# One weight chunk in four of the up stages split by two GpSimd transfers

## The chip, the cores and the metric

The kernel runs on one core of a Trainium2 chip. The core has a matmul engine (TensorE, PE in the profile; its weight loads are PEld), three engines for elementwise work (VectorE or DVE, ScalarE or ACT, GpSimd or POOL), an engine that mostly issues transfers (SyncE or SP), and 16 DMA engines that all issued transfers share. SBUF is the on-chip memory of 128 partitions, PSUM the banks that matmuls write. The metric is the device time of one execution in microseconds; lower is better.

## The reference

Two layers of a decoder on 256 tokens of width 1024, in float32. Each layer has a mixer (attention over the tokens and over a fixed memory) and then a channel mixer, the part that matters here:

```python
def _sq_relu_mlp(h, w_up, w_down):
    u = jax.nn.relu(h @ w_up)
    return (u * u) @ w_down
...
x = x + _sq_relu_mlp(_rmsnorm(x, a_norm_mlp[i]), a_w_up[i], a_w_down[i])
```

`w_up` is 1024 x 4096, `w_down` 4096 x 1024. Layer A's mixer is differential attention, layer B's a causal attention whose keys and values come from `w_kv`; a last norm follows.

## The kernel before

*Precision.* A float32 product is made of three passes in the type float32r, which TensorE takes in one pass each: an operand x is split into h, x rounded to float32r, and l = x - h, also rounded; the product is h·h + h·l + l·h. So every weight and every activation needs two instructions: a copy that rounds (ScalarE) and a subtraction (VectorE).

*Weight chunks.* All weights lie in `wall`, 192 chunks of 128 x 1024 floats (512 KB) in the order of use. `chunk()` (L319) takes the next: SP loads it into a `w` buffer (L313), ScalarE copies it rounded into a `wh` buffer (L336), VectorE subtracts into a `wl` buffer (L338). There are 4 `w`, 6 `wh` and 6 `wl` buffers, handed out strictly in the order in which the program names them.

*The up stage* (`mlp_up`, L777 on). 16 blocks b of two chunks (mi = 0, 1). `up_chunk` (L814) issues for a chunk 16 matmuls with `wh` (on `xn`'s h and l for each of 8 k) and then 8 with `wl` (L821), into one half of an `acc` bank (4 banks). After two chunks VectorE takes the bank through the relu and the norm's factor `rb` (L790), ScalarE squares (L793) and rounds it (L805), VectorE makes its l (L807). For the blocks 1, 3, 5, 7, 9 and 11 VectorE also makes four sums of blocks (L800 to L803), which the down stage uses.

*Around it.* Before the up stage lies the output projection (`out_proj`, L755, matmuls L765); when one of its banks is done, VectorE adds it to `xT` (L751), and `norm_tile` makes a piece of `xn` from that (ScalarE L352, VectorE L354); ScalarE squares the piece (L451) and GpSimd adds the squares up (L452), from which the norm's factor comes. After it comes the down stage (`natural_down`, matmuls L871), whose `fast_pair` trades an eighth of the products for more splits on ScalarE (L894) and VectorE (L895, L902).

*The order.* Every instruction is a step of a plan (`Plan`, L59). A step has an engine, an estimated duration, what it reads and writes, a `lag` (time after its end until the result can be used) and a priority, its place in the program minus a shift from a table (`EARLY`). `order()` (L118) plays the steps through with these estimates; each engine takes the ready step of the best priority whose buffers are free. The instructions are then issued in the order of the planned starts, and on the chip each engine works through its queue in that order, waiting where it must.

Of the kernel before, what the change touches and what calls it, by code (L numbers as in the profile page):

```python
# [26 lines left out]
CW = 1024  # L27
# [31 lines left out]
class Plan:  # L59
# [1 line left out]


    LAT = 200
    SAME = {"pe": 0, "act": 130, "dve": 130, "pool": 130, "dma": 0}

    def __init__(self, caps, fifo):
        self.caps = caps
# [48 lines left out]
        return st  # L116

    def order(self):  # L118
        look = {"pe": 0, "act": LOOK, "dve": LOOK, "pool": 0, "dma": 0}
        ready = {e: [] for e in self.SAME}  # L120
        idle = {e: 0 for e in self.SAME}
        idle["dma"] = 740
        events = []
        for st in self.steps:
            if st.wait == 0:
                for e, *_ in st.ways:
                    ready[e].append(st)
        heapq.heappush(events, 0)
        heapq.heappush(events, 740)
        releases = []  # L130
        port = 0
        left = len(self.steps)
        done = []
        while left:
            if not events:
                stuck = sorted((x.pri, e, [(b.cls, b.slot) for b in x.bufs]) for e in ready for x in ready[e])
                raise RuntimeError(f"plan stuck, {left} left: {stuck[:6]}")
            t = heapq.heappop(events)
            while events and events[0] <= t:
                heapq.heappop(events)  # L140
            while releases and releases[0][0] <= t:
                _, _, cls, slot = heapq.heappop(releases)
                self.free[cls].append(slot)
            for e in ready:
                if idle[e] > t or not ready[e]:
                    continue
                best, soon = None, None
                for st in ready[e]:
                    if st.start is not None:
                        continue  # L150
                    if not self.fits(st):
                        continue
                    if st.ready <= t:
                        if best is None or st.pri < best.pri:
                            best = st
                    elif st.ready <= t + look[e] and (soon is None or st.pri < soon.pri):
                        soon = st
                if best is None:
                    later = [st.ready for st in ready[e] if st.ready > t]
                    if later:  # L160
                        heapq.heappush(events, min(later))
                    continue
                way = next(x for x in best.ways if x[0] == e)
                if soon is not None and soon.pri < best.pri and t + way[1] > soon.ready + 100:
                    heapq.heappush(events, soon.ready)
                    continue
                st = best
                for e2, *_ in st.ways:
                    ready[e2].remove(st)
                st.start, st.end, st.eng, st.emit = t, t + way[1], e, way[2]  # L170
                if e == "pool" or (e == "dve" and st.port):
                    st.end = port = max(t, port) + way[1]
                for b in st.bufs:
                    if b.slot is None:
                        self.free[b.cls].sort()
                        b.slot = self.free[b.cls].pop(0)
                        if b.cls in self.fifo:
                            self.fifo[b.cls].remove(b)
                    b.left -= 1
                    if b.left == 0:  # L180
                        heapq.heappush(releases, (st.end + st.lag + self.LAT, id(b), b.cls, b.slot))
                        heapq.heappush(events, st.end + st.lag + self.LAT)
                idle[e] = st.end
                heapq.heappush(events, st.end)
                left -= 1
                done.append(st)
                for n in st.succ:
                    n.wait -= 1
                    same = len(n.ways) == 1 and n.ways[0][0] == e
                    n.ready = max(n.ready, st.end + st.lag + (self.SAME[e] if same else self.LAT))  # L190
                    if n.wait == 0:
                        for e2, *_ in n.ways:
                            ready[e2].append(n)
                        heapq.heappush(events, max(n.ready, t))
        self.span = max(st.end for st in done)
        return sorted(done, key=lambda x: x.start)
# [12 lines left out]
def t_act(n, psum=False, scale=False):  # L209
    return (51 if psum else 93) + 0.835 * n + (93 if scale else 0)  # L210
# [15 lines left out]
def tile_hybrid(ctx: ExitStack, tc: tile.TileContext, xa, xb, memt, xnat, mnat, w0, wall, consts, fgain, out):  # L226
# [17 lines left out]
    def buf(cls, shape, dt=F32, pool=None):  # L244
        pool = pool or ring
        return Buf(cls, lambda slot: pool.tile(shape, dt, name=name(cls), tag=f"{cls}{slot}", bufs=1))
# [72 lines left out]
    def chunk(dma_pieces=1):  # L319
        i = st_["i"]  # L320
        st_["i"] += 1
        w = buf("w", [128, CW])
        h = buf("wh", [128, CW], F32R)
        l = buf("wl", [128, CW], F32R)
        hs = (0, 1)
        if dma_pieces == 1:
            dma(lambda: w.t, wall[i], 4 * 128 * CW, w=[(w, 0), (w, 1)])
        else:
            for p in hs:
                dma(lambda p=p: w.t[:, p * 512:(p + 1) * 512], w0[p], 256 * CW, w=[(w, p)], pri=2 * p - 1.5)  # L330
        old, P.shift = P.shift, EARLY["w" + st_["layer"]]
        for p in (hs if st_["pieces"] == 2 else [hs]):
            q = p if isinstance(p, tuple) else (p,)
            sl = slice(q[0] * 512, q[-1] * 512 + 512)
            n = 512 * len(q)
            P.add(("act", t_act(n), lambda sl=sl: nc.scalar.copy(h.t[:, sl], w.t[:, sl])),  # L336
                  [(w, x) for x in q], [(h, x) for x in q])
            P.add(("dve", t_dve(n), lambda sl=sl: nc.vector.tensor_sub(l.t[:, sl], w.t[:, sl],  # L338
                                                                       h.t[:, sl].bitcast(F32))),
                  [(w, x) for x in q] + [(h, x) for x in q], [(l, x) for x in q], port=True)  # L340
        P.shift = old
        return h, l


    class Tiles:

# [427 lines left out]
    def mlp_up(st, sums=()):  # L774

        st.rstd()
        us = [big(i, [128, 4, 2, S], F32R) for i in range(8)]  # L777
        st_["pieces"] = 1
        first = True
        for b in range(16):  # L780
            u = buf("u", [128, 2, S])
            ps = bank("acc")
            for mi in range(2):
                wh, wl = chunk()
                up_chunk(ps, mi, wh, wl)
            if first:
                bcast(st)
                first = False
            k0 = 2 * b % 4
            P.add(("dve", t_dve(512, True), lambda u=u, ps=ps: nc.vector.scalar_tensor_tensor(  # L790
                u.t, ps.t.rearrange("p (a s) -> p a s", a=2), 0.0, rb_t[:, None, :].to_broadcast([128, 2, S]),
                op0=OP.max, op1=OP.mult)), [ps, "rb"], [u])
            P.add(("act", t_act(512), lambda u=u: nc.scalar.activation(u.t, u.t, AF.Square)), [u], [u])  # L793
            if b in sums:
                dst, keys = sums[b]

                def blocks(u=u, dst=dst):
                    a = [u.t[:, k, hf * 128:hf * 128 + 128] for hf in range(2) for k in range(2)]
                    s = [dst()[:, i * 128:i * 128 + 128] for i in range(4)]
                    nc.vector.tensor_add(s[0], a[2], a[3])  # L800
                    nc.vector.tensor_sub(s[1], s[0], a[0])
                    nc.vector.tensor_sub(s[2], a[0], a[2])
                    nc.vector.tensor_sub(s[3], a[1], s[1])  # L803
                P.add(("dve", 4 * t_dve(128) + 100, blocks), [u], keys, port=True)
            P.add(("act", t_act(512), lambda u=u, t=us[b // 2], k0=k0: nc.scalar.copy(t.t[:, k0:k0 + 2, 0], u.t)),  # L805
                  [u], [(us[b // 2], b)])
            P.add(("dve", t_dve(512), lambda u=u, t=us[b // 2], k0=k0: nc.vector.tensor_sub(  # L807
                t.t[:, k0:k0 + 2, 1], u.t, t.t[:, k0:k0 + 2, 0].bitcast(F32))), [u, (us[b // 2], b)],
                [(us[b // 2], b, 1)], port=True)
        return us  # L810
# [591 lines left out]
```

## Time and profile before

| | |
|---|---|
| three runs | 599.97 us median (599.6 to 600.78) |
| profiled execution, first to last instruction | 725.8 us |
| TensorE clock granted in it | 0.755 of full |
| busy in it: PE, DVE, ACT, POOL | 716.6, 491.3, 398.0, 54.4 us |
| up stages in it | 145.4 to 257.4 and 503 to 615 us |
| read from HBM | 106.72 MB |

The profiled execution has no time of its own beside its span; it is one execution at a lower TensorE clock than the timed ones can have had, as the span is longer than they took. A row of a group reads: line, engine, operation, output and inputs with shapes, count, then busy time and mean ns of one, then the idle time of the engine just before them and what ended it. In an order of time each row starts with start and duration in us, and ends with the idle time before it and its releaser in brackets.

### The profile page before, as it was taken

The page shows a single profiled execution, that of the slowest core. Times are in us where ns is not written, and L with a number is a line of the kernel's source. Part 1 is how long each engine was busy: PE and PEld are TensorE (multiplying, and loading weights), DVE is VectorE, ACT ScalarE, POOL GpSimd, SP SyncE. Part 2 cuts the span into 40 slices and gives each one's busy share as a digit, 9 for nine tenths or more (in the row PEclk, how much of TensorE's full clock was granted, in tenths as well). Part 3 has the DMA queues.
Part 4 walks back from the last instruction along what each step waited for, and adds up shares of the span by engine and source line. Part 5 has one row for each costly group of instructions (what it writes and reads, how often), then busy time and mean ns, then how long its engine had stood idle before and what let it go on. Part 6 is the DMA issues. An engine that isn't in the chain of part 4 may idle for free.

```text
span 725.8 us, 10368 instructions
## 1 busy us (share of the span) xinstructions
PE 716.6 (99%) x3794; PEld 590.5 (81%) x3794; DVE 491.3 (68%) x871; ACT 398.0 (55%) x750; POOL 54.4 (8%) x67
## 2 busy tenths in 40 slices
PE   9999999999999999999999999999999999999996
PEld 7676769999999977677777776889999999776775
DVE  5777666587556687766776577675675666876664
ACT  6776666455544554444575477656464455554422
POOL 0121110030000000000111121001200000000002
PEclk8777777777777777777777777777777777777777
DMA  8854432435444433546455432224444443354421
GB/s 303 293 183 165 146 95 79 145 119 175 151 168 146 152 139 132 188 145 209 139 174 179 169 120 85 88 88 143 153 164 152 154 158 125 127 186 151 148 85 59
DMA packets 30003, 108.45 MB, mean 149 GB/s; under 512 B 3328, under 2 KB 3328, under 8 KB 29696
## 3 DMA queue, kind: packets, MB, share of 16 engines
q1 hardware_dynamic: 29664, 107.26, 43.4%
q8 instruction: 30, 0.49, 0.3%
q10 hardware_dynamic: 288, 0.52, 0.2%
q14 instruction: 21, 0.17, 0.1%
HBM read 106.72 MB, written 1.05 MB: 148 GB/s over the span
## 4 chain that ended last, share of the span: by engine, by line
PE 98%; DVE 1%; DMA 1%; ACT 0%; issue 0%; SPq 0%; ACTq 0%
PE acc L821 30%; PE acc L499 23%; PE t L871 23%; PE acc L765 7%; PE acc L871 6%; PE t L586 2%; PE t L624 2%; PE t L681 1%; PE t L557 1%; DMA xT<-xa 1%; PE t L1013 0%; PE t L990 0%; DVE xT L751 0%; PE t L579 0%; PE t L721 0%; PE t L720 0%
## 5 line engine op out<-in xcount | busy, mean ns | idle before, releaser
L336 ACT CAST wh<-w 128x512 fp32r<-128x512 f32 (+1 forms) x232 | 182.5, 814 | 191.3 <-PE acc L821 74.0
L338 DVE TENSOR_TENSOR wl<-w,wh 128x512 fp32r<-128x512 f32 (+1 forms) x232 | 213.4, 939 | 86.7 <-ACT wh L336 71.7
L821 PE MATMUL acc<-xn,wh 128*128 128x256 f32 x1024 | 157.3, 314 | 0.5 <-DVE xn L354 0.5
L821 PEld LDWEIGHTS acc<-xn,wh 128*128 128x128 f32 x1024 | 150.7, 224 | 0.7 <-DVE xn L354 0.7
L871 PE MATMUL t<-wh,B 128*128 128x512 f32 (+1 forms) x368 | 134.4, 453 | 0.0
L499 PE MATMUL acc<-wh,xn 128*128 128x512 f32 x256 | 101.6, 472 | 0.7 <-ACT xn L352 0.7
L871 PEld LDWEIGHTS t<-wh,B 128*128 128x128 f32 x368 | 72.5, 199 | 29.8
L821 PE MATMUL acc<-xn,wl 128*128 128x256 f32 x512 | 84.1, 314 | 0.0
L871 PE MATMUL t<-wl,B 128*128 128x512 f32 (+1 forms) x184 | 82.9, 450 | 0.0
L821 PEld LDWEIGHTS acc<-xn,wl 128*128 128x128 f32 x512 | 78.1, 224 | 0.0
L499 PEld LDWEIGHTS acc<-wh,xn 128*128 128x128 f32 x256 | 51.0, 199 | 23.5 <-issue 2.2
L765 PE MATMUL acc<-B,wh 128*128 128x256 f32 x256 | 60.1, 323 | 0.0
L499 PE MATMUL acc<-wl,xn 128*128 128x512 f32 x128 | 58.0, 453 | 0.0
L790 DVE SCALAR_TENSOR_TENSOR u<-acc,rb 128x512 f32<-128x512 f32 x32 | 21.9, 690 | 50.5 <-PE acc L821 50.5
L871 PEld LDWEIGHTS t<-wl,B 128*128 128x128 f32 x184 | 37.0, 201 | 15.1
L765 PEld LDWEIGHTS acc<-B,wh 128*128 128x128 f32 x256 | 46.3, 216 | 0.9 <-issue 0.8
L452 POOL TENSOR_TENSOR sqa<-sqa,sq 128x256 f32<-128x256 f32 x21 | 20.3, 966 | 295.7 <-ACT sq L451 294.9
L765 PE MATMUL acc<-B,wl 128*128 128x256 f32 x128 | 40.0, 313 | 0.0
L895 DVE TENSOR_TENSOR wl<-wsum,wh 128x1024 fp32r<-128x1024 f32 x24 | 29.4, 1223 | 8.9 <-ACT wh L894 6.5
L533 POOL TENSOR_TENSOR ropet<-ropes,consts 128x256 f32<-128x256 f32 (+1 forms) x28 | 25.1, 917 | 129.0 <-ACT ropes L522 106.5
L499 PEld LDWEIGHTS acc<-wl,xn 128*128 128x128 f32 x128 | 26.8, 210 | 9.1
L894 ACT CAST wh<-wsum 128x1024 fp32r<-128x1024 f32 x24 | 25.3, 1052 | 15.9 <-PE acc L871 6.9
(223 smaller groups left out, 899.1 us busy)
## 6 DMA issues: line engine op xcount, KB each, us to landing
w<-wall SPq DMA_DIRECT2D x191, 512.0 KB, 3.3
w<-memt SPq DMA_DIRECT2D x4, 512.0 KB, 5.0
B<-xnat SPq DMA_DIRECT2D x1, 1024.0 KB, 7.4
B<-mnat SPq DMA_DIRECT2D x1, 1024.0 KB, 8.9
xT<-xa SPq DMA_DIRECT2D x1, 540.0 KB, 3.8
w<-w SPq DMA_DIRECT2D x2, 256.0 KB, 3.5
xT<-xb SPq DMA_DIRECT2D x1, 512.0 KB, 6.6
consts<-consts SPq DMA_DIRECT2D x1, 256.5 KB, 4.5
```

What stands on the lines that cost most here:

```text
L336: P.add(("act", t_act(n), lambda sl=sl: nc.scalar.copy(h.t[:, sl], w.t[:, sl])), [(w, x) for x in q], [(h, x) for x in q])
L338: P.add(("dve", t_dve(n), lambda sl=sl: nc.vector.tensor_sub(l.t[:, sl], w.t[:, sl], h.t[:, sl].bitcast(F32))), [(w, x) for x in q] + [(h, ...
L452: P.add(("pool", t_pool(S), lambda: nc.gpsimd.tensor_tensor(self.acc.t, self.acc.t, sq.t, op=OP.add)), [sq, self.acc], [self.acc])
L499: nc.tensor.matmul(pss[hf].t[:, c0:c1], a(k)[:, ts], b.t[:, o + c0:o + c1], start=(k == 0 and i == 0), stop=(k == KT - 1 and i == 2))
L533: nc.gpsimd.tensor_tensor(t.t[:, 0:nh, e:e + 32], zs.t[:, 0:nh, 32 - e:64 - e], b(sin[:, e:e + 32]), op=OP.mult)
L586: nc.tensor.matmul(sp[hd].t[:, c], qk[a].t[r, qb * 128:(qb + 1) * 128], qk[b].t[r, S:S + c.stop - c.start], start=(qb == 0 and i == 0 and ...
L765: nc.tensor.matmul(o, a.t[:, ws], x(k), start=(n == 0 and m % 2 == 0 and i == 0), stop=(n == KT - 1 and i == 2), skip_group_check=True)
L790: P.add(("dve", t_dve(512, True), lambda u=u, ps=ps: nc.vector.scalar_tensor_tensor(u.t, ps.t.rearrange("p (a s) -> p a s", a=2), 0.0, rb_ ...
L821: nc.tensor.matmul(ps.t[:, o], w.t[:, k * 128:(k + 1) * 128], xnt[:, k, x], skip_group_check=True, **flags)
L871: nc.tensor.matmul(ps.t[:, c0:c1], x, y, start=start and i == 0, stop=stop and i == 2, skip_group_check=True)
L894: P.add(("act", t_act(m), lambda: nc.scalar.copy(h[x].t[:, :m], src())), keys, [h[x]])
L895: P.add(("dve", t_dve(m), lambda: nc.vector.tensor_sub(l[x].t[:, :m], src(), h[x].t[:, :m].bitcast(F32))), keys + [h[x]], [l[x]], port=True)
```

## The change

In the odd blocks of both up stages the second chunk, so one in four, 16 in all, comes from a new function `added_chunk` instead of `chunk`. GpSimd issues a transfer of the chunk straight into the `wh` buffer (source float32, destination float32r, so it rounds). ScalarE multiplies `wh` by -1 into the `wl` buffer. GpSimd issues a second transfer of the same chunk that adds onto `wl`, which then holds the chunk less its rounded copy. No `w` buffer, no SP transfer and no subtraction on VectorE belong to such a chunk. In the plan the two transfers are steps of a queue of their own ("sw", 1300 ns each, lags 2500 and 3000), though they are issued on GpSimd's queue as its additions are. The steps of a chunk stay three.

```diff
-    SAME = {"pe": 0, "act": 130, "dve": 130, "pool": 130, "dma": 0}
+    SAME = {"pe": 0, "act": 130, "dve": 130, "pool": 130, "dma": 0, "sw": 0}
...
-        look = {"pe": 0, "act": LOOK, "dve": LOOK, "pool": 0, "dma": 0}
+        look = {"pe": 0, "act": LOOK, "dve": LOOK, "pool": 0, "dma": 0, "sw": 0}
...
+    def added_chunk():
+
+        i = st_["i"]
+        st_["i"] += 1
+        h = buf("wh", [128, CW], F32R)
+        l = buf("wl", [128, CW], F32R)
+        hk, lk = [(h, 0), (h, 1)], [(l, 0), (l, 1)]
+        P.add(("sw", 1300, lambda: nc.gpsimd.dma_start(h.t, wall[i])), (), hk, lag=2500)
+        old, P.shift = P.shift, EARLY["w" + st_["layer"]]
+        P.add(("act", t_act(CW), lambda: nc.scalar.mul(l.t, h.t.bitcast(F32), -1.0)), hk, lk)
+        P.shift = old
+        P.add(("sw", 1300, lambda: nc.gpsimd.dma_start(l.t, wall[i], accum_op=OP.add)), lk, lk, lag=3000)
+        return h, l
...
-                wh, wl = chunk()
+                wh, wl = added_chunk() if mi and b % 2 else chunk()
```

## The prediction

> **What bounds the kernel now.** I read the page's busy times, clock line and chain first, then the table of stages, then the waits inside an up stage, and last the order of time around one added chunk.
>
> ```profile
> span 725.8 us, 10368 instructions
> ...
> PE 716.6 (99%) x3794; PEld 590.5 (81%) x3794; DVE 491.3 (68%) x871; ACT 398.0 (55%) x750; POOL 54.4 (8%) x67
> ...
> PE 98%; DVE 1%; DMA 1%; ACT 0%; issue 0%; SPq 0%; ACTq 0%
> ...
> L336 ACT CAST wh<-w 128x512 fp32r<-128x512 f32 (+1 forms) x232 | 182.5, 814 | 191.3 <-PE acc L821 74.0
> L338 DVE TENSOR_TENSOR wl<-w,wh 128x512 fp32r<-128x512 f32 (+1 forms) x232 | 213.4, 939 | 86.7 <-ACT wh L336 71.7
> ```
>
> TensorE is busy for 716.6 of 725.8 us and 98% of the chain of work that ended last is its own; 9.2 us are all it idles. The two split instructions wait for others (last figures of their rows): the cast on ScalarE for TensorE to release a buffer, the subtraction on VectorE for the cast. The work that the change takes from VectorE is work that follows TensorE. The stages (window, length, then busy time and instructions of PE, PEld, DVE, ACT and POOL, granted clock, share of the DMA engines, GB/s):
>
> ```profile
> 145.40:165.50 20.10, 19.61 (x139) 19.38 (x138) 15.58 (x32) 11.41 (x21) 7.07 (x7) 0.75 0.37 132
> 165.50:257.40 91.90, 91.90 (x649) 91.90 (x649) 59.74 (x87) 46.55 (x58) 0.00 (x0) 0.75 0.47 155
> ...
> 523.10:615.00 91.90, 91.90 (x650) 91.90 (x649) 59.74 (x87) 46.31 (x58) 0.00 (x0) 0.75 0.46 155
> ```
>
> ```profile
> core 0: 725.8 us, clock 0.755
> ```
>
> The up stages are 145.4 to 257.4 and about 503 to 615. In their main stretches TensorE has no gap at all, VectorE is busy 65% and ScalarE 51%, and GpSimd does nothing. The granted clock was 0.755 (last row, the table of cores), and this is why the span says 725.8 while the runs took 599.97: TensorE's 716.6 us are 541 us at full clock (716.6 x 0.755). In the timed runs the clock must lie between 0.92 (541 over 599.97 less the 9.2 idle) and 1. I make the sum on the profiled execution as a difference and add it to 599.97; where a term depends on TensorE's pace I recompute it for clock 1. There VectorE's 59.74 us face 69.4 us of TensorE (91.90 x 0.755), 86%: still not the bound.
>
> **The change part by part.** Per added chunk (16 in all, 8 per up stage: every fourth) one SP transfer and one VectorE subtraction go; the cast on ScalarE becomes a multiplication by -1 of the same tile size; two GpSimd transfers of 512 KB come, one before and one after it. The groups, and below them a wait, in the first layer's main stretch (165.5 to 257.4):
>
> ```profile
> L338 DVE TENSOR_TENSOR wl<-w,wh 128x1024 fp32r<-128x1024 f32 x24 | 29.3, 1220 | 3.9 <-PE acc L821 2.7 <-ACT wh L336 0.7
> L336 ACT CAST wh<-w 128x1024 fp32r<-128x1024 f32 x23 | 24.2, 1051 | 29.5 <-PE acc L821 29.5
> ```
>
> ```profile
> DVE u L790 <- PE acc L821: 23.9, 12, 2.1
> ```
>
> *Subtraction removed:* 16 x 1.22 = 19.5 us off VectorE. In the main stretch VectorE then waits 8 x 1.22 us longer for TensorE; u (L790) already waits 23.9 us for TensorE's acc there. Worth to TensorE: 0. *Cast replaced:* 16 x 1.05 us out, the same in (nearest row: the cast itself; below it nothing, above it the 1.22 of the subtraction): 0, hidden under ScalarE's 29.5 us of waiting. *SP transfer removed:* the SP queue has 16 issues fewer; the next chunk's load takes the free w buffer earlier and then waits for TensorE as the cast did: 0.
>
> *Two transfers on GpSimd's queue.* The trace has none, so I bound them by the issue table (median us from issue to landing last).
>
> ```profile
> w<-wall SPq DMA_DIRECT2D x191, 512.0 KB, 3.3
> w<-memt SPq DMA_DIRECT2D x4, 512.0 KB, 5.0
> B<-xnat SPq DMA_DIRECT2D x1, 1024.0 KB, 7.4
> B<-mnat SPq DMA_DIRECT2D x1, 1024.0 KB, 8.9
> xT<-xb SPq DMA_DIRECT2D x1, 512.0 KB, 6.6
> ```
>
> The rounding transfer has the bytes and source of the first row: 3.3 to 6.6 us, and I take 4.2, between the rows of 3.3 and 5.0, as it is issued by another engine but in the same traffic. The adding transfer also reads its destination, so as many bytes again: 3.3 (the read is free) to 8.9 (the slowest 1 MB row), and I take 7.4, the other 1 MB row. What an issue takes of GpSimd itself has no row; it stands idle in the stretch (0.00 above), so it lengthens the chain at most. Extra traffic is 16 x 0.52 MB on 108, beside DMA engines that are 47% busy in the stage: 0. The Trainium skill, "Collectives: The Full Stack", section "The bandwidth ceiling", says that a reducing transfer is slower because the add needs two source reads, about half the rate; doubling the first row would make it 6.6 us and the chain below 11.9. No row here shows it, and the sum stays the same by either.
>
> What must hide them is the lead of the ring of six wh and six wl buffers (TensorE's and ScalarE's order of time, start and duration first, and a piece of the chain).
>
> ```profile
> 192.56 2.44 PE L821 MATMUL acc<-xn,wh 128*128 128x256 f32 x16
> 194.84 1.28 PE L821 MATMUL acc<-xn,wl 128*128 128x256 f32 x8
> ```
>
> ```profile
> 195.04 1.05 ACT L336 CAST wh<-w 128x1024 fp32r<-128x1024 f32 x1 [2.35 <-PE acc L821]
> ```
>
> ```profile
> 165.47 91.95 PE acc L821 x648
> ```
>
> A chunk is 24 matmuls, 16 with wh and then 8 with wl; 91.95 / 648 x 24 = 3.41 us. The cast at 195.04 starts just when a chunk's 16 wh matmuls end (192.56 + 2.44 = 195.0): a wh buffer comes free there, and it is read again by the sixth chunk after, whose wl is wanted six whole chunks later: 6 x 3.41 = 20.4 us, and 15.4 us at clock 1. Its wh is wanted 16 matmuls earlier, 18.2 and 13.7 us. The chain in that time is 4.2 + 1.05 + 7.4 = 12.7 us, at the low ends 7.7, at the high ends 16.6; its first half alone, at most 6.6, is far inside 13.7. Hidden, with 2.7 us left at clock 1. The multiplication waits on ScalarE's queue for the first transfer, with casts of the next chunks and u's squares behind it; they too have five chunks of lead, and four acc banks stand between u and TensorE. Cost 0.
>
> *GpSimd's queue.* The adding transfer waits there for ScalarE. Behind it can stand the adds of squares at the head of the stage.
>
> ```profile
> 155.12 1.49 POOL L452 TENSOR_TENSOR sqa<-sqa,sq 128x256 f32<-128x256 f32 x1 [0.56 <-ACT sq L451]
> ```
>
> ```profile
> POOL sqa L452 <- ACT sq L451: 294.9, 10, 196.2
> ```
>
> The last of them ends at 156.6 us, then GpSimd is idle for 196.2 us, so in the stage nothing is behind the transfers. At the head the adds feed the reciprocal root that u needs; u's first step runs some 10 us later, with TensorE in about its sixth chunk (145.4 + 6 x 3.41 = 165.9) and acc banks for eight: 7 us of room. Cost 0, at most a few tenths.
>
> *The head of the stage* is the one place without that lead.
>
> ```profile
> 139.84 1.05 ACT L336 CAST wh<-w 128x1024 fp32r<-128x1024 f32 x1 [2.08 <-PE acc L765]
> 143.23 1.05 ACT L336 CAST wh<-w 128x1024 fp32r<-128x1024 f32 x1 [2.34 <-PE acc L765]
> 144.54 1.36 ACT L352 ACTIVATE xn<-xT 128x256 fp32r<-128x256 f32 x3 [0.26 <-DVE xT L751]
> ...
> 495.91 1.05 ACT L336 CAST wh<-w 128x1024 fp32r<-128x1024 f32 x1 [2.34 <-PE acc L765]
> ```
>
> ```profile
> 149.79 3.79 PE L821 MATMUL acc<-xn,wh 128*128 128x256 f32 x25 [0.49 <-DVE xn L354]
> ```
>
> Casts of up chunks 0 to 5 run ahead of the stage; counted from the first, the one at 139.84 is chunk 3's, the first that is added. Its buffer is free at about 139.8; the multiplication can start when the transfer has landed, and 4.70 us after 139.84 ScalarE begins the eight xn pieces on which TensorE's first up matmuls wait (149.79: it does wait for xn, through VectorE). If the multiplication stands ahead of xn in ScalarE's order, xn is held once the transfer takes more than 4.70 - 1.05 = 3.65 us, at clock 1 more than 4.70 x 0.755 - 1.05 = 2.5. If it stands behind them nothing is held, as chunk 3's wl is wanted some 13 us into the stage. What is late next if xn comes later is VectorE's own run of adds and xn remainders, already continuous from 144.1 to 152.3, so it hides part. I take 0 here and carry the rest as a rival. The subtractions that fall away near the head (chunk 3's, right after 139.84, in idle time) give nothing either.
>
> Sum: 0 + 0 + 0 + 0: 725.8 for the profiled execution, **600.0** for the runs. What a measurement of this kernel tells from no change is about 0.2%, 1.2 us: 598.8 to 601.2.
>
> **The rivals.** *ScalarE is held at the head (slower).* At 4.2 us xn comes 0.55 us late per layer at the profile's clock and 1.7 at clock 1; at 6.6 us it is 2.95 and 4.1. Over two layers, with VectorE hiding none: 601.1 to 608.2, and 603.4 at my value and clock 1. For: the buffer frees only 4.70 us ahead of xn, in both layers. Against: order behind xn, or VectorE's own run. Beside it, the Trainium skill, "GPSIMD Engine Reference", section 2.1, says the first call of a freshly loaded GpSimd routine pays some 6 us; on the first transfer that would be about 9.3 us and would hold xn by up to 6.8 once. No row shows such a load.
>
> *The chain outlasts the ring (slower).* Decides at 15.4 us (clock 1). At the high ends, 16.6, each of 16 chunks is late by 1.2: 619; with 8.9 for both transfers 18.9, late by 3.5: 655. For: nothing like the adding transfer is in the trace. Against: it would have to take over 10 us for 512 KB, more than the slowest 1 MB row.
>
> *VectorE was a bound in the timed runs (faster).*
>
> ```profile
> 146.40:157.40 11.00, 10.51 (x75) 10.28 (x74) 8.79 (x14) 6.59 (x15) 7.07 (x7) 0.75 0.28 100
> 157.40:168.30 10.90, 10.90 (x80) 10.90 (x79) 8.56 (x20) 4.34 (x5) 0.00 (x0) 0.75 0.58 196
> 168.30:179.20 10.90, 10.90 (x79) 10.90 (x78) 8.47 (x17) 8.40 (x12) 0.00 (x0) 0.75 0.48 151
> ```
>
> ```profile
> 158.23 1.23 DVE L338 TENSOR_TENSOR wl<-w,wh 128x1024 fp32r<-128x1024 f32 x1 [2.21 <-PE acc L821]
> ```
>
> In the first 33 us VectorE is busy 78 to 80%; at clock 1 these windows are 8.2 to 8.3 us long and VectorE, with 8.5 to 8.8, is the longer. Two subtractions per layer (chunks 7 and 11; the one at 158.23 is of that time) leave it: at most 4 x 1.22 = 4.9, so 595.1; half of it, 597.5, if the ring hides the rest. A better order of the later stages, which the changed times also shift, would show the same sign. Against: the rings and banks let TensorE run on for five chunks, and 158.23 begins after a wait of 2.21.
>
> **How the numbers follow.** Hidden 0.38; held at the head 0.28; chain too long 0.09; VectorE was a bound 0.25. A slight holding within 1.2 us counts as no change (0.02 of the 0.28). So faster 0.25, same 0.40, slower 0.35. The forecast is the likeliest, 600.0, its own range 598.8 to 601.2. The range of 8 in 10 runs from 596.5, leaving 0.05 of the VectorE case, to 606.0, leaving the long chain (0.09) and the dearest part of the head (0.04).
>
> **What would show it.** Right: both up stretches still 91.9 us at the same clock, no idle time of PE L821 on wl, VectorE's busy time 19.5 us less and its waits longer by as much, GpSimd with 32 issues. Head right: the first xn on ScalarE still some 4.7 us after the third-last wh release. Wrong: PE idle before L821 with the new transfers as releaser (chain), ScalarE idle ahead of L352 until a GpSimd transfer (head), or shorter heads of both up stages (VectorE). A timed difference with equal profiles would put it on the clock that the profile doesn't have.

## The result: 1.4% slower, in the two up stages

The changed kernel took 606.91 us (median of 4 runs, 603.88 to 610.17), the kernel before 599.79 beside it (598.34 to 600.78): ratio 1.0136, 95% interval 1.0088 to 1.0183. The forecast was no change, 600.0, with a range up to 606.0, so it was wrong in kind and in size.

The profile of before on which the prediction rests had a granted clock of 0.755. A second profile of the same kernel, taken with the first experiments (c1), had 0.997 and belongs to a run of 597.4 us. Nearly all timed runs of before have clocks of 0.994 to 0.999, so it is the one to compare with. Page of that profile of before, first lines:

```profile
span 595.6 us, 10368 instructions
...
PE 582.2 (98%) x3794; PEld 513.2 (86%) x3794; DVE 485.2 (81%) x871; ACT 390.7 (66%) x750; POOL 56.0 (9%) x67
```

Page of the changed kernel (that run took 610.17 us), with the groups of the split instructions and the transfers (median us from issue to landing last):

```profile
span 608.4 us, 10367 instructions
...
PE 593.1 (97%) x3794; PEld 523.6 (86%) x3794; DVE 467.5 (77%) x855; ACT 387.6 (64%) x750; POOL 80.3 (13%) x99
...
L338 DVE TENSOR_TENSOR wl<-w,wh 128x512 fp32r<-128x512 f32 (+1 forms) x216 | 194.7, 924 | 48.7 <-ACT wh L336 48.1
L336 ACT CAST wh<-w 128x512 fp32r<-128x512 f32 (+1 forms) x216 | 164.9, 798 | 79.3 <-PE t L885 29.2
...
L354 ACT ACTIVATE wl<-wh 128x1024 fp32r<-128x1024 f32 x16 | 17.0, 1060 | 35.1 <-DMA wh<-wall 29.4
...
w<-wall SPq DMA_DIRECT2D x175, 512.0 KB, 4.3
wh<-wall POOLq DMA_DIRECT2D x16, 512.0 KB, 6.7
wl<-wall POOLq DMA_DIRECT2D x16, 512.0 KB, 5.7
```

(Up to L344 the changed kernel has the same line numbers; behind the new function every line stands 14 later, so the xn of L352 and L354 is L366 and L368, the up matmul L821 is L835, out_proj's L765 is L779. Inside the function L352 is the rounding transfer, L354 the multiplication by -1, L356 the adding transfer.)

VectorE has 17.7 us less to do, and TensorE is busy 10.9 us longer with the same 3794 matmuls. The 16 multiplications wait for their rounding transfers (29.4 us in all), whose landing takes 6.7 us in the median, not the 4.2 that the prediction took. Measured from the end of out_proj's last matmul to the first matmul of the down stage, the up stages are

| | layer A, us | layer B, us | rest of the span |
|---|---|---|---|
| before (at 0.997) | 89.54 | 90.10 | 416.0 |
| after | 93.10 | 97.54 | 417.8 |
| after, second and third profile | 94.73, 93.79 | 95.62, 96.73 | 414.7, 415.2 |

The rest of the span did not gain from VectorE's relief. In the first of these profiles 11.0 of the 12.8 us lie in the two up stages; the other 1.8 come ahead of the first added chunk, where TensorE waited 2.22 us at 32.67 us and the granted clock fell behind it (0.78, 0.50 and 0.87 in the windows of 2 us from 32 to 38), which before's profile does not have. In the second and third the up stages are longer by 10.7 and 10.9 us.

**The head.** Chain of the changed kernel, head of layer A's up stage and then of layer B's:

```profile
122.22 4.51 DMA wh<-wall
126.72 0.02 issue
126.75 1.06 ACT wl L354
127.81 0.41 ACT xn L366
...
414.93 7.04 DMA wh<-wall
421.96 0.02 issue
421.99 1.06 ACT wl L354
423.04 0.41 ACT xn L366
```

ScalarE's order of time there, layer B, after:

```profile
417.54 1.05 ACT L336 CAST wh<-w 128x1024 fp32r<-128x1024 f32 x1 [4.71 <-PE acc L779]
421.99 1.06 ACT L354 ACTIVATE wl<-wh 128x1024 fp32r<-128x1024 f32 x1 [3.40 <-DMA wh<-wall]
422.95 2.49 ACT L366 ACTIVATE xn<-xT 128x256 fp32r<-128x256 f32 x6
```

and in before at clock 0.997:

```profile
413.44 1.31 ACT L352 ACTIVATE xn<-xT 128x256 fp32r<-128x256 f32 x3
```

The multiplication of the first added chunk stands ahead of xn in ScalarE's queue, waits 3.40 us for its transfer, and xn with it. In before xn begins 1.7 us ahead of the end of out_proj (413.44 against 415.11; in layer A 124.32 against 125.98). In after it begins at its end in layer A (127.71 against 127.65) and 2.6 us behind it in layer B (422.95 against 420.38): held by 1.7 and 4.2 us. TensorE's order of time, after, layer A and layer B:

```profile
128.26 4.98 PE L835 MATMUL acc<-xn,wh 128*128 128x256 f32 x37 [0.61 <-ACT xn L366]
...
423.49 4.52 PE L835 MATMUL acc<-xn,wh 128*128 128x256 f32 x22 [2.23 <-ACT xn L366]
```

After the gap in layer B the granted clock itself falls (table of windows; the figure ahead of the last two is the clock):

```profile
420.00:424.00 4.00, 1.64 (x13) 1.21 (x11) 0.98 (x4) 2.01 (x4) 0.65 (x1) 1.00 0.20 69
424.00:428.00 4.00, 3.98 (x22) 3.85 (x23) 4.00 (x9) 3.95 (x11) 2.01 (x3) 0.71 0.74 131
428.00:432.00 4.00, 4.00 (x32) 4.00 (x31) 1.95 (x3) 3.10 (x6) 2.08 (x3) 0.87 0.42 133
```

Windows of half a us show how: the clock is at one half from about 425.7 to 429.1 us, some 3.4 us, and full before and behind. Its two ends:

```profile
425.50:426.00 0.50, 0.50 (x5) 0.50 (x5) 0.50 (x3) 0.50 (x3) 0.00 (x0) 0.65 0.86 147
...
428.50:429.00 0.50, 0.50 (x4) 0.50 (x3) 0.50 (x2) 0.10 (x1) 0.42 (x2) 0.50 0.30 41
429.00:429.50 0.50, 0.50 (x6) 0.50 (x5) 0.50 (x1) 0.50 (x2) 0.42 (x1) 0.94 0.90 213
```

4 x 0.29 + 4 x 0.13 = 1.7 us of matmul time are lost there beside the 2.2 of waiting.

**The step.** The long pieces of the chain in the main stretches, before at clock 0.997:

```profile
142.23 73.45 PE acc L821 x648
...
431.92 73.46 PE acc L821 x648
```

and after:

```profile
144.82 76.09 PE acc L835 x646
...
441.76 76.32 PE acc L835 x648
```

There is no gap in either and the clock is 1.00 in both, yet a matmul comes every 113.3 ns (73.45 / 648) in before and every 117.8 in after: 2.9 us per stretch. So in this profile the 11.0 us are 5.7 for this step, and what is left, 0.7 in layer A and 4.6 in layer B, is the head's: in layer B 2.2 of waiting and 1.7 of clock make most of it (in layer A before had waited 1.05 us for VectorE anyway). The split is this execution's: the step comes out otherwise in others, before's included (below).

### The profile page after: what moved, and what is told of

Read it like the earlier page. It is cut to its first block, busy times and chain, and to the rows that moved or that the text cites. A ratio compares the mean times of both kernels' runs of the same rounds, so it can differ in the third digit from the quotient of the medians.

```text
span 608.4 us, 10367 instructions
## 1 busy us (share of the span) xinstructions
PE 593.1 (97%) x3794; PEld 523.6 (86%) x3794; DVE 467.5 (77%) x855; ACT 387.6 (64%) x750; POOL 80.3 (13%) x99
## 3 DMA queue, kind: packets, MB, share of 16 engines
HBM read 115.11 MB, written 1.05 MB: 191 GB/s over the span
## 4 chain that ended last, share of the span: by engine, by line
PE 90%; DMA 5%; ACT 2%; DVE 2%; issue 1%; SPq 0%; ACTq 0%
PE acc L835 29%; PE t L885 22%; PE acc L513 19%; PE acc L885 6%; PE acc L779 6%; PE t L600 2%; DMA wh<-wall 2%; PE t L638 2%; DMA w<-wall 2%; PE t L695 1%; DMA w<-memt 1%; PE t L571 1%; DVE wl L338 1%; DVE xn L368 1%; DMA xT<-xa 1%
## 5 line engine op out<-in xcount | busy, mean ns | idle before, releaser
L338 DVE TENSOR_TENSOR wl<-w,wh 128x512 fp32r<-128x512 f32 (+1 forms) x216 | 194.7, 924 | 48.7 <-ACT wh L336 48.1
L336 ACT CAST wh<-w 128x512 fp32r<-128x512 f32 (+1 forms) x216 | 164.9, 798 | 79.3 <-PE t L885 29.2
L835 PE MATMUL acc<-xn,wh 128*128 128x256 f32 x1024 | 134.1, 283 | 3.5 <-ACT xn L366 2.8
L835 PEld LDWEIGHTS acc<-xn,wh 128*128 128x128 f32 x1024 | 126.4, 190 | 4.8 <-ACT xn L366 3.3
L885 PE MATMUL t<-wh,B 128*128 128x512 f32 (+1 forms) x368 | 111.9, 386 | 0.0
L513 PE MATMUL acc<-wh,xn 128*128 128x512 f32 x256 | 86.2, 404 | 0.8 <-ACT xn L366 0.6
L835 PE MATMUL acc<-xn,wl 128*128 128x256 f32 x512 | 70.5, 280 | 0.0
L835 PEld LDWEIGHTS acc<-xn,wl 128*128 128x128 f32 x512 | 64.6, 189 | 0.0
L779 PE MATMUL acc<-B,wh 128*128 128x256 f32 x256 | 50.8, 289 | 0.0
L807 ACT ACTIVATE u<-u 128x512 f32<-128x512 f32 x32 | 20.2, 630 | 40.0 <-DVE u L804 40.0
L779 PEld LDWEIGHTS acc<-B,wh 128*128 128x128 f32 x256 | 41.1, 191 | 0.6 <-issue 0.5
L354 ACT ACTIVATE wl<-wh 128x1024 fp32r<-128x1024 f32 x16 | 17.0, 1060 | 35.1 <-DMA wh<-wall 29.4
L779 PE MATMUL acc<-B,wl 128*128 128x256 f32 x128 | 36.1, 282 | 0.0
L821 DVE TENSOR_TENSOR B<-u,B 128x512 fp32r<-128x512 f32 x32 | 22.0, 687 | 13.8 <-ACT B L819 13.8
L619 ACT ACTIVATE B<-t,nm 128x128 f32<-128x128 f32 (+1 forms) x64 | 27.2, 443 | 4.6 <-DVE nm L615 2.7
```

The costliest lines, as they stand in the source:

```text
L354: P.add(("act", t_act(CW), lambda: nc.scalar.mul(l.t, h.t.bitcast(F32), -1.0)), hk, lk)
L513: nc.tensor.matmul(pss[hf].t[:, c0:c1], a(k)[:, ts], b.t[:, o + c0:o + c1], start=(k == 0 and i == 0), stop=(k == KT - 1 and i == 2))
L619: nc.scalar.activation(p[hd].t[:, c], sp[hd].t[:, c], AF.Exp, bias=nm[hd][:, qb:qb + 1], accum_out=ss[:, hd, qb:qb + 1])
L779: nc.tensor.matmul(o, a.t[:, ws], x(k), start=(n == 0 and m % 2 == 0 and i == 0), stop=(n == KT - 1 and i == 2), skip_group_check=True)
L835: nc.tensor.matmul(ps.t[:, o], w.t[:, k * 128:(k + 1) * 128], xnt[:, k, x], skip_group_check=True, **flags)
L885: nc.tensor.matmul(ps.t[:, c0:c1], x, y, start=start and i == 0, stop=stop and i == 2, skip_group_check=True)
```

## The experiments

Ratios are to the kernel before on the same chip, which took 596.93 (first four rows), 597.6 (e4, e5), 598.55 (e7, e8) and 597.49 us (last three).

| run | us | ratio, 95% interval |
|---|---|---|
| e1 multiplication behind xn | 611.43 | 1.0244 (1.0210 to 1.0279) |
| e2 without the first added chunk | 599.03 | 1.0025 (1.0006 to 1.0044) |
| e3 only the first added chunk | 604.55 | 1.0117 (1.0086 to 1.0148) |
| c1 before, profiled | 597.4 | one run |
| e4 plan with longer landings | 607.58 | 1.0162 (1.0122 to 1.0203) |
| e5 before, ScalarE held | 606.67 | 1.0137 (1.0106 to 1.0169) |
| e6, e9 after; c2 before | 606.83, 607.51; 595.89 | one run each |
| e7 before, eight interruptions | 603.97 | 1.0095 (1.0063 to 1.0126) |
| e8 subtractions away | 600.89 | 1.0042 (1.0017 to 1.0067) |
| e10 before, one interruption a stage | 602.74 | 1.0068 (1.0034 to 1.0102) |
| e12 before, two a stage | 602.21 | 1.0058 (1.0027 to 1.0088) |
| e11 after, one a stage | 605.32 | 1.0117 (1.0066 to 1.0167) |

**Which chunk costs it: e2 and e3.** The 16 added chunks are parted into the first of each stage and the other 14.

```diff
-                wh, wl = added_chunk() if mi and b % 2 else chunk()
+                wh, wl = added_chunk() if mi and b % 2 and b > 1 else chunk()   # e2
+                wh, wl = added_chunk() if mi and b == 1 else chunk()            # e3
```

> The first added chunk of each up stage goes through the old path, 14 stay. Head theory: 598 to 601, the second added chunk's transfer has the whole ring as its lead. Even theory and traffic theory: 14/16 of the loss stays, about 606.

> Only the first added chunk of each up stage, 2 in all. Head theory: 604 to 608, nearly all of the loss, with xn late in both layers. Even theory and traffic theory: 2/16 of the loss, about 600.7.

Without the first one the kernel is 0.25% slower than before; the first one alone costs 1.2%. Together 1.4%, as measured. In e2 both heads are those of before (TensorE waits for xn only 1.1 us, in layer A, on VectorE), and its up stages are 90.57 and 90.37 us, so 1.0 and 0.3 us longer. In e3 the head of layer B is held again, by a wait of 2.0 us. Its up stages are 89.89 and 96.90 us: nearly all of the loss is in layer B, where the main stretch also runs at the slow step (75.85 us for 644 matmuls), so e3's 1.2% is not the head alone.

**The other order: e1.** A longer lag for the first rounding transfer puts the multiplication behind xn.

```diff
-        P.add(("sw", 1300, lambda: nc.gpsimd.dma_start(h.t, wall[i])), (), hk, lag=2500)
+        P.add(("sw", 1300, lambda: nc.gpsimd.dma_start(h.t, wall[i])), (), hk, lag=9000 if late else 2500)   # late: b == 1
```

> All 16 added chunks stay; only the first one of each up stage gets a longer lag in the plan (9000 in place of 2500), which puts its multiplication behind the xn pieces in ScalarE's order. Head theory (ScalarE's queue is held at the head of each up stage by the first transfer, some 7 us in all): 599 to 601, the first xn within 1 us of its add in both layers, no TensorE gap there. Even theory (each of the 16 chunks costs about 0.45 us through the chain or through traffic): 606 to 607, unchanged. Traffic theory (the SP loads are slowed by the adding transfers): 606 to 607.

A miss: it is slower by another percent. xn is early again (123.15 us, out_proj ends at 124.82), but now the adding transfer is late. GpSimd's order of time in layer A, e1:

```profile
119.39 0.74 POOL L352 DMA_DIRECT2D wh<-wall  x1 [3.42 <-PE acc L779]
125.17 1.55 POOL L466 TENSOR_TENSOR sqa<-sqa,sq 128x256 f32<-128x256 f32 x2 [5.04 <-ACT sq L465]
128.78 3.48 POOL L466 TENSOR_TENSOR sqa<-sqa,sq 128x256 f32<-128x256 f32 x2 [2.07 <-ACT sq L465]
132.21 0.89 POOL L356 DMA_DIRECT2D wl<-wall  x1
```

and TensorE's:

```profile
141.18 2.08 PE L835 MATMUL acc<-xn,wl 128*128 128x256 f32 x8 [4.45 <-DMA wl<-wall]
```

The adding transfer is issued at 132.21 behind the adds of squares, which wait for ScalarE, and lands 8.9 us later (the median in this run is 5.6); TensorE stands 4.45 us for it. Ahead of xn the first added chunk holds xn, behind it its own wl is late: neither order was free.

**A plan with longer landings: e4.** The plan's two transfers get other issue times and lags: the rounding one now takes 7.0 us in the plan (measured in after: 6.7 in the median), the adding one 8.5, which is nearer to the 8.9 of e1's head than to the median of 5.7.

```diff
-        P.add(("sw", 1300, lambda: nc.gpsimd.dma_start(h.t, wall[i])), (), hk, lag=2500)
+        P.add(("sw", 600, lambda: nc.gpsimd.dma_start(h.t, wall[i])), (), hk, lag=6400)
...
-        P.add(("sw", 1300, lambda: nc.gpsimd.dma_start(l.t, wall[i], accum_op=OP.add)), lk, lk, lag=3000)
+        P.add(("sw", 900, lambda: nc.gpsimd.dma_start(l.t, wall[i], accum_op=OP.add)), lk, lk, lag=7600)
```

> All 16 added chunks, with the durations and lags of the two transfers in the plan set to what the first trace shows (600 + 6400 and 900 + 7600 in place of 1300 + 2500 and 1300 + 3000), nothing else. If the head loss comes of the order alone (multiplication ahead of xn, and in the run with the multiplication behind xn TensorE's wl matmuls too early in its queue): 597 to 601. If the adding transfer at the head can't be in time in any order: 603 or more, with TensorE waiting for wl there.

The wait for xn at the head is gone, and the time is not: three waits for wl (1.9 us together), two for u (1.5) and one for the adds of squares (0.7) took its place, and the slow step came in parts of both stretches. The profiled run is the quickest of six (605.21 us). With these lags the chain had no room; whether lags nearer to the medians would do better was not tried.

**The hold without the transfers: e5.** In before, the cast of the same chunk is done six times over, so ScalarE is held, and no transfer is changed.

```diff
-            P.add(("act", t_act(n), lambda sl=sl: nc.scalar.copy(h.t[:, sl], w.t[:, sl])),
+            P.add(("act", t_act(n), lambda sl=sl: [nc.scalar.copy(h.t[:, sl], w.t[:, sl]) for _ in range(times)]),   # times: 6 if b == mi == 1
```

> The kernel before, no GpSimd transfer; only the cast of the fourth chunk of each up stage is done six times on ScalarE (five for nothing), which ends some 2.7 us after the time at which xn would start. Head theory (what costs is that xn is held on ScalarE): 601 to 608, TensorE stalls of 1 to 3 us at both heads. Rival (the transfers themselves cost): 597 to 600, since the five casts fall into idle time of ScalarE. If the slow step of TensorE (118 in place of 113 ns per matmul for a whole up stage) follows a disturbed head, at least one of the two up stages has it here.

It is as slow as the changed kernel. Waits, windows and chain of e5, and between them VectorE's row ahead of xn:

```profile
PE acc L821 <- ACT xn L352: 5.8, 2, 2.9
```

```profile
125.98 1.23 DVE L338 TENSOR_TENSOR wl<-w,wh 128x1024 fp32r<-128x1024 f32 x1 [6.86 <-ACT wh L336]
```

```profile
128.00:132.00 4.00, 3.73 (x17) 3.18 (x18) 4.00 (x10) 4.00 (x11) 1.47 (x2) 0.77 0.40 133
132.00:136.00 4.00, 3.99 (x28) 3.70 (x28) 4.00 (x7) 2.20 (x6) 2.57 (x4) 0.80 0.40 131
424.00:428.00 4.00, 4.00 (x24) 4.00 (x23) 4.00 (x8) 4.00 (x11) 1.85 (x3) 0.61 0.56 199
```

```profile
145.86 73.45 PE acc L821 x648
...
440.75 73.46 PE acc L821 x648
```

Holding xn costs TensorE 2.9 us per stage in waiting and more in clock after it (stages 93.92 and 95.30 us: +4.4 and +5.2). The main stretches keep the fast step: a hold at the head does not make the slow one by itself. So e5 shows that a held xn alone can cost this much, but not that it costs it in after: the hold is larger here, 4.0 us in both layers against 1.7 and 4.2, and it goes by VectorE too, whose subtraction of that chunk waits 6.86 us for the casts with the adds onto xT behind it.

**VectorE: e8.** The 16 subtractions are left out of before; the wl matmuls of these chunks read wh, so that part of the product is left out.

```diff
-        l = buf("wl", [128, CW], F32R)
+        l = h if less else buf("wl", [128, CW], F32R)   # less: mi and b % 2; then no subtraction
```

> The kernel before without the 16 subtractions on VectorE and without anything in their place: for every fourth chunk of the up stages the wl matmuls read wh instead, so the second part of these products is left out. No GpSimd transfer. Theory that the relief of VectorE is worth nothing here: 596 to 599, within 0.3% of before, the up stages 89.5 and 90.1 us long. VectorE theory (it was a bound at this clock): 592 to 595.

No gain: in its profile the span is 595.6 us and the up stages 89.52 and 90.10, as in before, so VectorE was no bound and the relief was worth nothing. That profile is of the quickest of its twelve runs (597.35 us); the median is 0.4% above before's, not within the 0.3% expected, and why is open.

**After and before again: c1, c2, e6, e9.**

> The kernel before, unchanged, for a profile at the clock of the timed runs: 600 us. Head theory: at the heads of both up stages no gap of TensorE above 1 us, and the granted clock stays at 1 there. If VectorE was a bound in the timed runs, TensorE has gaps ahead of L821 or L871 in the first 30 us of the up stages.

> The kernel before once more, for the same question: 596 to 601; 113 ns in both up stages at 597, one stage at 118 if it takes about 600.

> The changed kernel again for a second profile: 603 to 611. If TensorE's step in the up stages (118 or 113 ns) is a matter of chance per execution, it can come out otherwise than in the first profile, and the time then moves by some 2.9 us per stage; if it follows from the kernel, both stages have 118 again.

> The changed kernel a third time, for its profile: 603 to 611. Held-head theory: xn starts on ScalarE after the last matmul of the output projection in both layers, and the up stages are 3 to 8 us longer than before's 89.5 and 90.1. If 118 ns is tied to this kernel's order, both stages have it; by chance per execution, one or none may.

Both profiles of before run all main stretches at the fast step (c2's stages are 89.54 and 90.11 us). After is slow in both stages in e9, and in e6 in most of layer A's but not in layer B's, where the stage is 5.5 us longer than before's all the same. The head is held in all three profiles of after: 2.8, 3.1 and 2.8 us of waits for xn. The steady chain is late now and then (e6):

```profile
PE acc L835 <- DMA wl<-wall: 1.8, 2, 1.2
```

**What sets the step: e7, e10, e12, e11.** In the profiles the step changes where the run of up matmuls is broken: by the two small products for the norm's factor (one-column matmuls on `sqa`, then the product with `dg`), by a wait, and a few times by a hitch of 0.14 us with no cause in the trace (e6, at 160 us). Between such places it stays. Before has both steps too: in c1 the 38 matmuls between the two small products run at 117.8, the stretch behind them at 113.3. So pairs of one-column matmuls into a spare bank were put in: after blocks 4, 7, 10 and 13 (e7), after block 0 (e10, and e11 in the changed kernel), after blocks 0 and 1 (e12).

```diff
+            if b in (4, 7, 10, 13):
+                tp = bank("t")
+                P.add(("pe", 220, lambda tp=tp: [nc.tensor.matmul(tp.t[:, h:h + 1], ones, ones[:, 0:1], start=h == 0,
+                                                                 stop=True, skip_group_check=True) for h in range(2)]),
+                      [(us[b // 2], b)], [tp])
```

> The kernel before with a pair of one-column matmuls (about 0.4 us) into a spare bank after blocks 4, 7, 10 and 13 of each up stage, nothing else. Step theory (TensorE has two steps in the up stages, 113 and 118 ns per matmul, and an interruption of the stream of weight-loaded matmuls can move it from one to the other): some of the stretches between the interruptions run at 118, and the time is 3 us (the eight interruptions alone) to 8 us above before. Rival (118 ns needs the GpSimd transfers or a held head): 113 ns in every stretch, 600 to 603.

The chain of e7 in layer A:

```profile
140.82 16.33 PE acc L826 x144
157.50 17.07 PE acc L826 x144
174.91 16.43 PE acc L826 x144
191.68 17.07 PE acc L826 x144
```

Every pair flips the step: 113.4, 118.5, 114.1, 118.5 ns per matmul, and the same alternation in layer B, eight flips by eight pairs.

> The kernel before with one pair of one-column matmuls into a spare t bank after block 0 of each up stage, a few us into the main stretch. Theory (the pair flips TensorE's step between 113 and 118 ns per matmul, and the step stays until the next interruption): both main stretches run at the slow step, about 76 us instead of 73.45 for some 648 matmuls, so +2.6 us per stage and +0.36 for each pair: about +5.9 us, ratio 1.010. Rival (an interruption costs its own time only): +0.7 us, ratio 1.001, and both stretches stay at 73.45.

> The kernel before with such a pair after block 0 and another after block 1 of each up stage, some 5 us apart. Theory (each flips the step): slow for two chunks or so between the pairs, fast in the rest: +4 x 0.36 and a few tenths, about +2 us, ratio 1.003, less than with one pair although there are twice as many. Rival (the slow pace comes from having interruptions at all, and does not go back): as with one pair or more, +6 us and over, ratio 1.010 or more. Rival (own time only): +1.4, ratio 1.002, with no stretch at the slow step.

> The kernel after with one such pair after block 0 of each up stage. In the three profiles of the kernel after, about five of the six main stretches began at the slow step. Theory (a flip): most of them run at the fast step now, some 4 of 6 stretches less on balance, 2.6 us each over two stages gives -3.5 us, and +0.7 for the pairs: about -2.8 us against the kernel after, so a ratio of 1.008 to 1.010 to the kernel before, where the kernel after had 1.0136; the wait for xn at the head (2 to 4 us per layer) stays. Rival (own time only): +0.7 us, ratio about 1.015.

The main stretches behind the pairs, in the chains of e10, of e12 and of e11:

```profile
145.60 71.72 PE acc L826 x608
...
439.17 71.24 PE acc L826 x604
```

```profile
146.70 70.77 PE acc L826 x600
...
440.23 68.12 PE acc L826 x600
```

```profile
146.91 68.56 PE acc L840 x604
...
440.99 62.78 PE acc L840 x532
```

One pair leaves before slow in both layers (118.0 ns). Its cost, 0.7%, is some six times the 0.7 us that the two pairs take themselves, so the step and not the interruption is what costs. Two pairs did not bring the fast step back in both layers: 118.0 ns in A, 113.5 in B, and 0.6% slower, not the 0.3% of a plain flip. They came 8 and 4 matmuls apart, not the 5 us that was expected, so e12 does not test a return from a settled slow stretch. In the changed kernel one pair turned layer A fast (113.5) and left layer B slow (118.0); its ratio of 1.0117 cannot be told from the 1.0136 without it. (The expectation counts five slow beginnings among the six main stretches of after; there were four.) In e10's and e11's layer B the stretch was slow before the pair and stayed slow. So an interruption can change the step, and did in ten of the twelve pairs of e7, e10 and e11, but it is no switch that can be set. What decides it was not found. Of the 23 runs of before itself on the chip of the last three rows, 21 lie between 595.4 and 604.0 us; a step that falls differently in each execution would do that, but both its profiles are of quick runs, so that is not shown.

## Why the prediction was wrong

*The failed step is the head.* "I take 0 here and carry the rest as a rival": the rival is what happened, with the mechanism as described. The prediction put the term at 0 although its own 4.2 us for the transfer gave 1.7 us a layer at clock 1. The rival's formula at clock 1, the transfer less 2.5 us, gives 2.0 and 4.5 us for the transfers of 4.51 and 7.04 at the two heads; held were 1.7 and 4.2. The choice between the orders need not have been left open either: the plan's numbers decide it, and by a hair. Played through with the kernel's own estimates, the plan starts the first rounding transfer of layer A at 117.25 us, has the multiplication ready 1300 + 2500 + 200 ns later, at 121.25, and the first piece of xn at 121.39, so the multiplication goes first; in layer B the margin is 0.14 us too.

*The size of the rounding transfer* (4.2 taken, 3.3 to 6.6 given) was too low: the median measured is 6.7, just outside the range, and the two at the heads took 4.51 and 7.04. The adding transfer was over-priced, 7.4 against a measured 5.7; the two errors had opposite signs, so the chain's 12.7 was near the measured 6.7 + 1.06 + 5.7 = 13.5, while the head hangs on the first half alone. By the half rate that the Trainium skill, "Collectives: The Full Stack", section "The bandwidth ceiling", gives for a reducing transfer (measured there in collectives), the adding transfer would take about twice a plain load; here it took 5.7 us beside 4.3 for the plain one.

*"If it stands behind them nothing is held"* was wrong as well (e1): wl is wanted 13 us into the stage, but GpSimd's queue keeps the adding transfer behind adds that wait for ScalarE.

*Late next.* VectorE's own run hid part in layer A (1.7 us held, 0.7 more in the stage), and nothing in layer B, where before has no gap. The lower clock after the gap was not in the sum, nor was the slow step; with the hold's 5.9 us alone the rival's time would have been 605.9, which lies near the measured 606.91 partly by luck, as in layer A most of the hold was hidden and the clock and the step made up for it.

*The scaling to clock 1* was off as well. The prediction multiplied TensorE's times by 0.755: 91.95 us would become 69.4. The same 648 matmuls took 73.45 at full clock (c1), and TensorE's 541 us were 582.2. So VectorE was busy 59.27 of 73.45 us there, 81% and not 86, and the ring's lead was some 16.3 us (6 x 24 matmuls of 113.3 ns), not 15.4.

*Right:* the subtraction is worth nothing (e8), and the cast and the freed SP transfers brought no gain that shows (e2, with 14 added chunks, is not faster than before; the rest of the span is unchanged); the ring hides most of the steady chain (e2: 0.25%, not the 1.2 us per chunk of the long-chain rival); VectorE was no bound. The 6 us that the Trainium skill's "GPSIMD Engine Reference", section 2.1, gives for a first call do not show: the first rounding transfer landed in 4.51 us, the quickest of the 16.

*The signs to look for.* The wait of ScalarE until a GpSimd transfer and GpSimd's 32 issues came as listed. That both stretches keep their length at the same clock did not come, and a longer stretch without a gap was in none of the cases.

## What to carry to other kernels

A new chain through a ring of buffers is priced at the ring's steady lead and again where the ring starts anew: there its first instruction sits in an in-order queue ahead of what the next stage waits for. If the price there is "transfer less a margin", and the margin lies inside the transfer's own range, zero is not the value to take; play the plan through to see which order it will choose, and by how much. A transfer of a new kind deserves a wider range than the plain ones of its size give: the rounding transfer landed in 4.5 to 7.9 us here, past the 6.6 of the slowest plain row.

## What was not expected of the hardware

TensorE ran the same 128x256 matmuls at 113.3 or at 117.8 ns each at a granted clock of 1.00, for a whole stretch of 650, and the step changed only where that stream was broken: 2.9 us per stage that no wait shows, only TensorE's busy time and the length of a piece of the chain.

A gap of 2.2 us was followed by a granted clock of 0.71 and 0.87 over the next two windows of 4 us (after), one of 2.9 us by 0.77 and 0.80, and 0.61 (e5). In all profiles but the first of before, every wait of TensorE of 1.8 us or more (eleven, the shortest 1.82 in e2) was followed by such a fall, no wait of up to 1.3 us was, and between them it went either way: 1.52 and 1.68 fell (layer B of e9 and of e11), 1.49, 1.52 and 1.76 did not (early in c1, e1 and e8). A fall cost about 1.7 us of matmul time beside the wait itself (after, e5). The Trainium skill, "TensorE: Matmul & The Clock Gate", Part 1, puts the drop after an idle window of about 3.4 us; most of the gaps here are shorter and the clock fell all the same.

GpSimd itself is busy 576 ns for each rounding and 873 ns for each adding transfer that it issues, in the same queue as its adds.
